# TensorE's order written by hand from the trunk to the first up tiles of an encoder layer

## The chip, the cores and the metric

The kernel runs on one core of one Trainium2 chip. The metric is the device time of one execution in microseconds (us); the time of a version is the median of its runs. An engine executes its own queue in order; queues wait for each other through semaphores.

## What is computed

One layer of a hybrid streaming encoder for 1024 prompt frames and 32 sample frames, model width 1024, all in float32:

```python
def trunk_layer(x, ...):                       # x: frames x 1024
    z = rms_norm(x, g_mix) @ w_in              # q, k, v, conv_h, conv_B, conv_C, gate_a, gate_b
    a = window_attention(q, k, v) @ w_attn_out
    bo = (cb * causal_conv3(cc * ch)) @ w_conv_out
    x = x + (sigmoid(ga) * a + sigmoid(gb) * bo) @ w_mix_out
    cq = rms_norm(x, g_cross) @ w_cq           # 4 heads x 64, 256 memory tokens
    x = x + softmax_attention(cq, mem_k, mem_v) @ w_co
    x = x + square(relu(rms_norm(x, g_mlp) @ w_up)) @ w_down
    return x                                   # then a final rms_norm
```

`rms_norm(x, g)` is `x * rsqrt(mean(x*x) + 1e-6) * g`.

## The kernel before

**Layout and precision.** Activations lie transposed: 128 features on the partitions, frames along the free axis. The 1056 frames are cut into three chunks `CH` of 384, 384 and 288 frames, called c = 0, 1, 2 here. Every float32 operand is split in two float32r parts, hi and lo; a product is then three matmuls (hi·hi, hi·lo, lo·hi) for each of 8 feature blocks, 24 matmuls in `gemm`. A weight tile (128 x 1024) is loaded raw into `wr`, its hi part `wh` is copied by ScalarE (ACT), its lo part `wl` is subtracted by VectorE (DVE). Outputs go to PSUM: three `acc` tiles, two `pt` tiles, one `s` and one `o`.

**Weights.** `plan` is a list of items; `worder` is the order of their weights. `next_w` keeps up to three split weights ahead. `fetch_w` lets SyncE (SP) load the raw tile; there are two `wr` tiles, so a load waits until the tile two before it has been split. From the trunk on each weight is used once per chunk, so three times. For every second tile of `w_conv_out`, `w_mix`, `w_cq`, `w_co` and `w_up` (the dictionary `kept`, 14 tiles) the lo part is written to DRAM (`wl_d`) by a DMA from ACT's queue when it is first made, and loaded back the two later times instead of being subtracted anew.

**Order of the work around the change.** For chunk c the trunk is 16 products: `do_conv_out(c, f)` for f = 0..7, whose results are split into `mg` (tiles M), and `do_mix(c, f)` for f = 0..7, which adds to the residual `x1`, makes the operands of the cross attention (`gain_split`), and adds the squares up in `accs[c]` (`square_acc`, on GpSimd, POOL). Beside the trunk of chunk c+1 runs the cross attention of chunk c, in small steps: statistics (`chunk_stats`), two products `do_cq`, for each head `scores`, `turn` (transposes of the probabilities) and `values`, then `do_co` in two halves, and statistics again. The statistics are two parts: `stats_col` sums the squares with TensorE (into `pq`) and takes the inverse root on DVE and ACT; `stats_row` builds diagonal matrices on ACT (L207) and DVE (L208) and spreads the result over the partitions with TensorE (`pr`, L209 and L210); ACT copies it to `R[c]`. The cross attention of chunk 2 runs beside the up products of chunks 0 and 1 (`up0(0) + up0(1)`); then come the up products of chunk 2 for the first 8 of 32 hidden blocks. Chunks 0 and 1 are normalised ahead of the up products (`normed_split`); chunk 2's up products take the raw rows, and `R[2]` is multiplied in when the product leaves PSUM. The other 24 hidden blocks are done in 12 pairs (`up_pair`), which multiply two chunks and two blocks with seven half products on sums of operands (`combine_n`, `combine`); the raw weights of a pair are `r1` (in `wr`) and `r2` (in `wr2`, two tiles). At last comes the down product.

`beside(steps, fillers, late)` interleaves: after each filler product one step of the cross attention is put. It sets the order in the program's text. The order in each engine's queue is then set by a scheduler at build time, which goes through the program with estimated durations and gives an engine the first instruction, by place in the text, whose inputs are there by then: a matmul of a later product may come ahead of a statistic that is not ready by the estimate. Only the loads at the start are exempt (`manual_schedule` for SP).

Of the kernel before, what the change touches and what calls it, by code (L numbers as in the profile page):

```python
# [10 lines left out]
F32 = mybir.dt.float32  # L11
F32R = mybir.dt.float32r
AF = mybir.ActivationFunctionType
ALU = mybir.AluOpType
# [4 lines left out]
P = 128  # L19
# [4 lines left out]
NF = 8  # L24
KV = 4
EPS = 1e-6
NCT = 6


G_MIX, G_CROSS, G_MEM, G_MLP, G_FIN = 0, 8, 16, 24, 32  # L30
# [8 lines left out]
def hybrid_step(ctx: ExitStack, tc: tile.TileContext, io):  # L39
# [5 lines left out]
    def nm(s):  # L45
        uid[0] += 1
        return f"{s}_{uid[0]}"
# [12 lines left out]
    wp = ctx.enter_context(tc.tile_pool(name="wp", bufs=3))  # L60
# [29 lines left out]
    def tmp(n, dt=F32):  # L90
        return tp.tile([P, n], dt, tag="ct", bufs=NCT, name=nm("ct"))

# [10 lines left out]
    def item(fn, *keys):  # L103
        plan.append((fn, keys))
        worder.extend(keys)
# [18 lines left out]
    fetched = []  # L124

    def fetch_w():
        raw = wp.tile([P, 1024], F32, tag="wr", bufs=2, name=nm("wr"))
        sp.dma_start(raw, weight(worder[wpos[0] + len(fetched)]))
        fetched.append(raw)

    def issue_w():
        if not fetched:
            fetch_w()
        raw = fetched.pop(0)
        key = worder[wpos[0]]
        hi = wp.tile([P, 1024], F32R, tag="wh", name=nm("wh"))
        lo = wp.tile([P, 1024], F32R, tag="wl", name=nm("wl"))
        if kept.get(key) is not None:
            sp.dma_start(lo.bitcast(F32), kept[key])
            act.copy(hi, raw)  # L140
# [81 lines left out]
    def chunk_stats(c):  # L222
        chunk_col(c)
        chunk_row(c)
# [711 lines left out]
    def hidden(c, j, h):  # L936
        sp.dma_start(hid_d[c][:, j], h)

    def up_part(w, c, j):
        n = CH[c][1]  # L940
        a = ps.tile([P, n], F32, tag="pt", bufs=2, name=nm("pa")) if w[0] == "late" else acc_tile([P, n])
        gemm(a, w[-2:], xm[c])
        t = tmp(n)
        if c == 2:
            dve.scalar_tensor_tensor(t, a, 0.0, R[c], op0=ALU.max, op1=ALU.mult)  # L945
        else:
            dve.tensor_scalar_max(t, a, 0.0)
        h = tmp(n)
        pool_e.tensor_tensor(h, t, t, op=ALU.mult)
        hidden(c, j, h)  # L950

    def do_up(j, c):
        return (lambda w: up_part(w, c, j)), ("w_up", j)


    comb = {}
# [34 lines left out]
    raws, wset = {}, {}  # L991

    def pair_fetch(key, src1, src2):
        r1 = wp.tile([P, 1024], F32, tag="wr", bufs=2, name=nm("wr"))
        r2 = L["pool"].tile([P, 1024], F32, tag="wr2", bufs=2, name=nm("wr2"))
        sp.dma_start(r1, src1)
        sp.dma_start(r2, src2)
        raws[key] = [r1, r2]

    def pair_issue(key, which):  # L1000
        r1, r2 = raws[key][:2]
# [28 lines left out]
    def up_fetch(i):  # L1030
        if i < len(UP):
            pair_fetch(("u", i), io["w_up"][UP[i][0]], io["w_up"][UP[i][1]])

    def up_issue(i, which):
        if i < len(UP):
# [100 lines left out]
        return x  # L1136


    def cross_steps(c):
        units = [Cross(c, h) for h in ([0, 1, 2, 3] if c < 2 else [4, 0, 1, 2, 3])]  # L1140
        nu = len(units)
        steps = [("call", [mem_load] if c == 0 else [mem_load_s] if c == 1 else [])]
        steps.append(("call", [lambda: chunk_stats(c)]))
        steps.append(("items", [(do_cq(c, j), ("w_cq", j)) for j in range(2)]))
        for i in range(nu + 2):
            calls = []
            if i < nu:
                calls.append(units[i].scores)
            if 0 <= i - 2 < nu:
                calls.append(units[i - 2].values)  # L1150
            if 0 <= i - 1 < nu:
                calls.append(units[i - 1].turn)
            steps.append(("call", calls))
            if c < 2 and i < nu:
                steps.append(("call", []))
        if c == 2:
            steps.append(("call", [open_late]))
            steps.append(("call", []))
            steps.append(("call", []))
        steps.append(("items", [(do_co(c, 0), ("w_co", 0))]))  # L1160
        steps.append(("items", [(do_co(c, 1), ("w_co", 1))]))
        steps.append(("call", [lambda: chunk_stats(c)]))
        return steps

    def beside(steps, fillers, late=()):
        for i, filler in enumerate(fillers):
            item(*filler)
            for x in [x for at, x in late if at == i]:
                item(lambda x=x: x())
            if steps:  # L1170
                kind, what = steps.pop(0)
                for x in what:
                    if kind == "items":
                        item(*x)
                    else:
                        item(lambda x=x: x())
        return steps

    def trunk(c):
        return [(do_conv_out(c, f), ("w_conv_out", f)) for f in range(NF)] + [  # L1180
# [6 lines left out]
    left = beside([], trunk(0))  # L1187
    left = beside(cross_steps(0), trunk(1))

    normed = lambda c, at: [(at + i, lambda f=f: normed_split(c, f)) for i, f in enumerate((0, 4, 1, 5, 2, 6, 3, 7))]  # L1190
    left = beside(left + cross_steps(1), trunk(2), normed(0, 6))
    left = beside(left + cross_steps(2), up0(0) + up0(1), normed(1, 0) + [(4, lambda: combine_n(0)), (6, lambda: combine_n(1)), (8, lambda: combine_n(2)), (9, lambda: combine_n(3))])
    assert not left
    for j in range(NF):
        item(*do_up(j, 2))
        if j < 4:
            item(lambda j=j: combine(j))
        if j == 5:
            item(lambda: [up_fetch(0), up_fetch(1), up_issue(0, 1)])
        if j == 6:  # L1200
            item(lambda: [up_issue(0, 2), up_issue(1, 1)])


    worder.append(STOP)
# [67 lines left out]
    def final_last(c):  # L1272

        n = CH[c][1]
        for f in range(NF):
            act.mul(x1[c][f], x1[c][f], col(G_FIN + f))
        chunk_col(c)
        row = stats_row(BLOCKS[c], n, RC[c])
        r = misc.tile([P, n], F32, tag=f"R{c}", name=nm("R"))
        act.copy(r, row)  # L1280
        at = 0
        for k, tag in ((1, "wr"), (2, "wh"), (2, "wl"), (3, "wr")):
            y = wp.tile([P, k, n], F32, tag=tag, bufs=2 if tag == "wr" else 3, name=nm("y"))
# [135 lines left out]
```

## Time and profile before

| | before |
|---|---|
| median of 3 runs | 1846.12 us (1845.42 to 1847.79) |
| profiled execution, time | 1845.38 us |
| profiled execution, span from first to last instruction | 1843.6 us |
| TensorE busy, matmuls | 1802.2 us, 11364 |
| VectorE, ScalarE, GpSimd busy | 1048.8, 720.6, 363.1 us |
| mean granted TensorE clock | 0.993 |

Engines in the profile: PE is TensorE, PEld its weight loads, DVE is VectorE, ACT ScalarE, POOL GpSimd, SP SyncE; a trailing q is the engine's sequencer. L166 is line 166 of the kernel. In the view by stages a row is a stretch of time in us from the span's start; its columns are the length, the busy time of PE, PEld, DVE, ACT and POOL with the number of instructions, the mean granted clock of TensorE as a share of full speed, the busy share of the DMA engines and GB/s. In the timeline a row is start, duration, engine, line, operation, written tile <- read tiles, count, and in brackets the idle time of the engine before it and who ended it.

In the trace the trunk of chunk 0 runs from about 816 to 884 us, that of chunk 1 to about 972, that of chunk 2 to about 1066, the up products of chunks 0 and 1 to about 1169, those of chunk 2 to about 1202; the pairs follow.

### The profile page before, as it was taken

To read this page: it belongs to the slowest core of one execution; us is meant where nothing else is said; L and a number is where in the kernel's file an instruction comes from. 1 tells how busy PE (TensorE), PEld (TensorE's weight loads), DVE (VectorE), ACT (ScalarE), POOL (GpSimd) and SP (SyncE) were. 2 spreads that over 40 slices of the span, in tenths; PEclk is the share of its full clock that TensorE was granted. 3 is DMA by queue.
4 is the path that set the end of the run, shared out by engine and by line. 5 is a ranking of instruction groups with operands and counts; after the bars stand their busy time and mean duration, and the time that the engine had idled before them with its cause. 6 is when DMAs were issued, how large, how long until landed. Compare 5 with 4: busy or idle time off the path is not lost.

```text
span 1843.6 us, 29554 instructions
## 1 busy us (share of the span) xinstructions
PE 1802.2 (98%) x11364; PEld 1785.2 (97%) x11364; DVE 1048.8 (57%) x2011; ACT 720.6 (39%) x1414; POOL 363.1 (20%) x381
## 2 busy tenths in 40 slices
PE   7999999999999999999999999899999999999997
PEld 7999999999999999999999999799999999999997
DVE  7766767757664223336675967646555664242255
ACT  7643435435344102323555746522222443030134
POOL 3211010201100000004333333463443000000023
PEclk9999999999999999999999999899999999999999
DMA  4411111212123124236755767733232674131244
GB/s 176 140 64 59 62 55 59 70 56 70 56 94 106 58 94 149 73 121 226 248 186 202 244 213 236 265 124 105 100 108 86 205 234 142 45 116 46 70 142 147
DMA packets 113933, 232.76 MB, mean 126 GB/s; under 512 B 13536, under 2 KB 76672, under 8 KB 113664
## 3 DMA queue, kind: packets, MB, share of 16 engines
q1 hardware_dynamic: 109472, 220.38, 36.0%
q10 hardware_dynamic: 4320, 10.49, 1.5%
q8 instruction: 90, 1.47, 0.3%
q14 instruction: 51, 0.42, 0.1%
HBM read 184.34 MB, written 46.48 MB: 125 GB/s over the span
## 4 chain that ended last, share of the span: by engine, by line
PE 89%; DVE 4%; DMA 3%; ACT 2%; issue 2%; SPq 0%; POOL 0%; POOLq 0%; DVEq 0%; ACTq 0%
PE acc L166 22%; PE acc L167 22%; PE acc L168 22%; PE acc L1024 3%; PE acc L1025 3%; PE acc L1026 3%; PE pt L535 1%; PE pa L168 1%; PE pa L167 1%; PE pa L166 1%; DVE wl L115 1%; PE sc L510 1%; PE sc L509 1%; PE o L548 1%; PE o L547 1%
## 5 line engine op out<-in xcount | busy, mean ns | idle before, releaser
L114 ACT CAST wh<-wr 128x1024 fp32r<-128x1024 f32 x200 | 210.6, 1053 | 485.6 <-PE acc L167 381.8
L166 PE MATMUL acc<-X,wh 128*128 128x384 f32 (+1 forms) x1200 | 391.0, 326 | 8.5 <-ACT wh L114 8.0
L167 PE MATMUL acc<-X,wh 128*128 128x384 f32 (+1 forms) x1200 | 388.1, 323 | 0.9 <-DVE X L241 0.9
L168 PE MATMUL acc<-X,wl 128*128 128x384 f32 (+1 forms) x1200 | 387.0, 323 | 0.3 <-DVE wl L115 0.3
L166 PE MATMUL acc<-Y,wh 128*128 128x384 f32 (+1 forms) x1008 | 330.2, 328 | 7.6 <-DVE ct L945 4.1
L167 PE MATMUL acc<-Y,wh 128*128 128x384 f32 (+1 forms) x1008 | 329.2, 327 | 0.0
L168 PE MATMUL acc<-Y,wl 128*128 128x384 f32 (+1 forms) x1008 | 328.8, 327 | 0.0
L115 DVE TENSOR_TENSOR wl<-wr,wh 128x1024 fp32r<-128x1024 f32 x200 | 268.4, 1342 | 78.7 <-ACT wh L114 77.8
L166 PEld LDWEIGHTS acc<-X,wh 128*128 128x128 f32 x1200 | 226.5, 189 | 9.2 <-ACT wh L114 8.0
L167 PEld LDWEIGHTS acc<-X,wh 128*128 128x128 f32 x1200 | 226.6, 189 | 2.7 <-DVE X L241 2.1
L168 PEld LDWEIGHTS acc<-X,wl 128*128 128x128 f32 x1200 | 226.4, 189 | 0.8 <-DVE wl L115 0.8
L166 PEld LDWEIGHTS acc<-Y,wh 128*128 128x128 f32 x1008 | 192.6, 191 | 9.0 <-DVE ct L945 4.3
L167 PEld LDWEIGHTS acc<-Y,wh 128*128 128x128 f32 x1008 | 192.4, 191 | 0.0
L168 PEld LDWEIGHTS acc<-Y,wl 128*128 128x128 f32 x1008 | 192.2, 191 | 0.0
L237 POOL TENSOR_TENSOR xacc<-xacc,ct 128x384 f32<-128x384 f32 (+1 forms) x62 | 82.2, 1329 | 358.0 <-ACT ct L235 355.5
L166 PE MATMUL acc<-M,wh 128*128 128x384 f32 (+1 forms) x320 | 104.8, 329 | 1.7 <-DVE Gb L761 1.7
L168 PE MATMUL acc<-M,wl 128*128 128x384 f32 (+1 forms) x320 | 104.5, 327 | 0.6 <-DVE wl L115 0.6
L167 PE MATMUL acc<-M,wh 128*128 128x384 f32 (+1 forms) x320 | 104.4, 327 | 0.2 <-DVE M L115 0.2
L747 POOL TENSOR_TENSOR ct<-ct,ld 128x384 f32<-128x384 f32 (+1 forms) x21 | 23.8, 1138 | 372.0 <-DVE ct L746 344.4
L1135 DVE TENSOR_TENSOR Gb<-acc,Gb 128x384 f32<-128x384 f32 (+1 forms) x60 | 31.4, 523 | 111.2 <-PE acc L168 111.2
L114 ACT CAST PTh<-pt 128x512 fp32r<-128x512 f32 (+3 forms) x94 | 45.9, 518 | 122.8 <-PE pt L535 122.0
L166 PE MATMUL acc<-H,wh 128*128 128x288 f32 (+1 forms) x256 | 80.7, 315 | 0.0
(292 smaller groups left out, 3482.6 us busy)
## 6 DMA issues: line engine op xcount, KB each, us to landing
wr<-in_w_down SPq DMA_DIRECT2D x56, 512.0 KB, 3.3
wr<-in_w_in SPq DMA_DIRECT2D x50, 512.0 KB, 3.2
wr<-in_w_up SPq DMA_DIRECT2D x48, 512.0 KB, 3.8
wl<-wl_d SPq DMA_DIRECT2D x28, 512.0 KB, 4.4
wr<-in_w_conv_out SPq DMA_DIRECT2D x24, 512.0 KB, 4.5
wr<-in_w_mix SPq DMA_DIRECT2D x24, 512.0 KB, 4.6
ct<-hid_d SPq DMA_DIRECT2D x64, 192.0 KB, 3.8
hid_d<-lt SPq DMA_DIRECT2D x48, 192.0 KB, 1.8
```

Of the source, the lines that this page charges most:

```text
L114: act.copy(hi, src)
L115: dve.tensor_sub(lo, src, hi.bitcast(F32))
L166: pe.matmul(out, wh[:, a], hi, start=(k == 0), stop=False)
L167: pe.matmul(out, wh[:, a], lo, start=False, stop=False)
L168: pe.matmul(out, wl[:, a], hi, start=False, stop=(k == len(acts) - 1))
L237: pool_e.tensor_tensor(acc, acc, sq, op=ALU.add)
L509: pe.matmul(sc[:, h, j * w : j * w + w], q[h], a, start=True, stop=False)
L747: (dve if f == NF - 1 else pool_e).tensor_tensor(t, t, t1, op=ALU.add)
L1024: pe.matmul(acc, wh[:, a], hi, start=(start and k == 0), stop=False, skip_group_check=True)
L1025: pe.matmul(acc, wh[:, a], lo, start=False, stop=False, skip_group_check=True)
L1026: pe.matmul(acc, wl[:, a], hi, start=False, stop=(k == 3), skip_group_check=True)
L1135: dve.tensor_add(x, a, x)
```

## The change

- TensorE's queue is taken out of the scheduler's hands from the first product of the trunk to the last of the first 24 up products (`manual_schedule` for PE): there it follows the text. The other engines are ordered by the scheduler as before.
- `beside` and the lists of steps are replaced by one list of 56 fillers (the trunks of chunks 1 and 2, and the up products of chunks 0, 1 and 2) and a table `after_filler`, which says by number what comes after which filler. Chunk c's cross attention starts at filler 0, 16, 32.
- The two parts of a statistic stand one filler apart (`chunk_col` after filler 0, 16, 32, 48; `chunk_row` after 1, 17, 33, 49), where `chunk_stats` had them together. After 16 and 32 two chunks have their parts together.
- `values` comes one filler after `turn` for every head; for chunks 0 and 1 it was two fillers for the first three heads. `turn` comes two fillers after `scores`; for chunk 2 it was one. Chunk 2's five heads start after fillers 35, 36, 38, 39 and 41 (they started after 35 to 39).
- `normed_split(0, f)` stands after fillers 18 to 25 (it was 22 to 29), `normed_split(1, f)` after 34 to 39 (32 to 39), `combine_n` after 40 to 43 (36 to 41), `combine` after 49 to 52 (48 to 51).
- The first two up products of chunk 2 leave their PSUM tiles only after `R[2]` is there (`all_waiting`); their matmuls don't wait for it.
- Raw weights have three tiles (`NWR`) in place of two, in the whole kernel. In the pairs `r1` and `r2` share those three; `wr2` keeps one tile for the first pair, loaded earlier (`up_first`).
- The 14 lo parts are written to DRAM from SP's queue in place of ACT's.

```diff
+NWR = 3
...
-        raw = wp.tile([P, 1024], F32, tag="wr", bufs=2, name=nm("wr"))
+        raw = wp.tile([P, 1024], F32, tag="wr", bufs=NWR, name=nm("wr"))
...
-                act.dma_start(kept[key], lo.bitcast(F32))
+                sp.dma_start(kept[key], lo.bitcast(F32))
...
-    def up_part(w, c, j):
+    def up_part(w, c, j, wait=False):
         n = CH[c][1]
         a = ps.tile([P, n], F32, tag="pt", bufs=2, name=nm("pa")) if w[0] == "late" else acc_tile([P, n])
         gemm(a, w[-2:], xm[c])
+        def rest():
+            t = tmp(n)
+            if c == 2:
+                dve.scalar_tensor_tensor(t, a, 0.0, R[c], op0=ALU.max, op1=ALU.mult)
...
+        if wait:
+            waiting.append(rest)
         else:
+            rest()
...
-        r1 = wp.tile([P, 1024], F32, tag="wr", bufs=2, name=nm("wr"))
-        r2 = L["pool"].tile([P, 1024], F32, tag="wr2", bufs=2, name=nm("wr2"))
+        r1, r2 = (wp.tile([P, 1024], F32, tag="wr", bufs=NWR, name=nm("wr")) for _ in range(2))
...
+    def up_first(step):
+        if step == 0:
+            L["rest"] = pair_fetch_first(("u", 0), io["w_up"][UP[0][0]], io["w_up"][UP[0][1]])
+        else:
+            L["rest"]()
...
+    def cross_steps(c, base, starts, co_at, stats_at):
         units = [Cross(c, h) for h in ([0, 1, 2, 3] if c < 2 else [4, 0, 1, 2, 3])]
+        at(base, lambda: chunk_col(c))
+        at(base + 1, lambda: chunk_row(c))
+        for j in range(2):
+            at(base + 2, (do_cq(c, j), ("w_cq", j)))
+        for i in range(base, base + 16):
+            for lag, step in ((3, "values"), (2, "turn"), (0, "scores")):
+                if i - base - lag in starts:
+                    at(i, getattr(units[starts.index(i - base - lag)], step))
+        for j in range(2):
+            at(base + co_at + j, (do_co(c, j), ("w_co", j)))
+        at(base + stats_at, lambda: chunk_col(c))
+        at(base + stats_at + 1, lambda: chunk_row(c))
...
+    in_order = tc.manual_schedule(engines={mybir.EngineType.PE})
+    item(lambda: in_order.__enter__())
+    for filler in trunk(0):
+        item(*filler)
+    at(0, mem_load)
+    cross_steps(0, 0, [3, 5, 7, 9], 13, 16)
+    at(16, mem_load_s)
+    cross_steps(1, 16, [3, 5, 7, 9], 13, 16)
+    cross_steps(2, 32, [3, 4, 6, 7, 9], 13, 16)
+    at(44, open_late)
+    at(49, all_waiting)
+    for i, f in enumerate((0, 4, 1, 5, 2, 6, 3, 7)):
+        at(18 + i, lambda f=f: normed_split(0, f))
+        at((34, 35, 35, 36, 37, 37, 38, 39)[i], lambda f=f: normed_split(1, f))
+    for k in range(4):
+        at(40 + k, lambda k=k: combine_n(k))
+        at(49 + k, lambda k=k: combine(k))
+    at(50, lambda: up_first(0))
+    at(53, lambda: [up_first(1), up_fetch(1), up_issue(0, 1)])
+    at(54, lambda: [up_issue(0, 2), up_issue(1, 1)])
+    run_fillers(trunk(1) + trunk(2) + up0(0) + up0(1) + up0(2))
+    item(lambda: in_order.__exit__(None, None, None))
```

More of the change, by code (lines that the diff above doesn't have):

```diff
@@ L998, in pair_fetch, with pair_fetch_first, rest @@
         raws[key] = [r1, r2]
+    def pair_fetch_first(key, src1, src2):
+        r2 = L["pool"].tile([P, 1024], F32, tag="wr2", name=nm("wr2"))
+        sp.dma_start(r2, src2)
+        def rest():
+            r1 = wp.tile([P, 1024], F32, tag="wr", bufs=NWR, name=nm("wr"))
+            sp.dma_start(r1, src1)
+            raws[key] = [r1, r2]
+        return rest
     def pair_issue(key, which):
@@ L1136, in down_part, with at @@
         return x
-    def cross_steps(c):
+    after_filler = {}
+    def at(i, *what):
+        after_filler.setdefault(i, []).extend(what)
+    def cross_steps(c, base, starts, co_at, stats_at):
         units = [Cross(c, h) for h in ([0, 1, 2, 3] if c < 2 else [4, 0, 1, 2, 3])]
[L1141 to L1163, printed above, removed]
@@ L1166, in beside, with run_fillers @@
+        at(base + stats_at, lambda: chunk_col(c))
+        at(base + stats_at + 1, lambda: chunk_row(c))
+    def run_fillers(fillers):
         for i, filler in enumerate(fillers):
             item(*filler)
[L1168 to L1176, printed above, removed]
@@ L1177, in beside @@
-        return steps
+            for x in after_filler.get(i, ()):
+                if isinstance(x, tuple):
+                    item(*x)
+                else:
+                    item(lambda x=x: x())
     def trunk(c):
@@ L1186, in hybrid_step @@
         kept.update(((name, j), None) for j in range(1, n, 2))
[L1187 to L1201, printed above, removed]
+    in_order = tc.manual_schedule(engines={mybir.EngineType.PE})
[20 more added lines that the diff above has]
+    item(lambda: in_order.__exit__(None, None, None))
     worder.append(STOP)
```

21 lines of the change are left out of this document (11 added, 10 removed).

## The prediction

> **What bounds the kernel now.** I read the page first, then the view by stages, then the waits of TensorE, then the timeline at its longest waits. From the page:
>
> ```profile
> span 1843.6 us, 29554 instructions
> PE 1802.2 (98%) x11364; PEld 1785.2 (97%) x11364; DVE 1048.8 (57%) x2011; ACT 720.6 (39%) x1414; POOL 363.1 (20%) x381
> ```
>
> TensorE works for all but 41.4 us of the span, and the change alters no matmul. So there is nothing to win but idle time and time at a lowered clock. The stages show where these lie (length, PE, PEld, DVE, ACT, POOL busy, granted clock, DMA share, GB/s):
>
> ```profile
> 0.00:816.00 816.00, 804.61 (x5179) 795.37 (x5180) 462.79 (x1081) 333.09 (x750) 85.49 (x154) 1.00 0.25 85
> 816.00:884.00 68.00, 67.24 (x381) 66.22 (x380) 43.54 (x55) 26.90 (x41) 26.77 (x19) 1.00 0.68 228
> 884.00:972.00 88.00, 88.00 (x525) 87.89 (x524) 60.46 (x102) 51.18 (x95) 25.83 (x23) 1.00 0.62 206
> 972.00:1066.00 94.00, 88.07 (x598) 86.80 (x597) 67.85 (x132) 58.65 (x115) 35.46 (x33) 0.96 0.65 218
> 1066.00:1169.00 103.00, 97.34 (x588) 94.00 (x587) 75.69 (x145) 56.95 (x124) 36.24 (x29) 0.98 0.74 250
> 1169.00:1202.00 33.00, 26.83 (x163) 25.96 (x164) 20.08 (x33) 14.47 (x24) 18.88 (x17) 0.84 0.74 238
> 1202.00:1240.00 38.00, 36.38 (x234) 35.82 (x233) 18.14 (x21) 9.42 (x12) 24.88 (x20) 1.00 0.30 99
> 1240.00:1843.60 603.60, 593.76 (x3708) 593.11 (x3706) 300.26 (x446) 169.91 (x258) 109.58 (x90) 0.99 0.36 119
> ```
>
> Length less PE is the idle time: 11.4 us before the trunk, 9.8 us in the last stage, and between them, where the order is now laid by hand, 0.8 + 0 + 5.9 + 5.7 + 6.2 + 1.6 = 20.1 us. The clock is below full only where idle time is. Narrower stretches price that, and give the length of a product:
>
> ```profile
> 990.30:997.10 6.80, 6.78 (x24) 6.79 (x25) 5.77 (x17) 2.39 (x7) 2.39 (x3) 0.51 0.60 230
> 1080.30:1086.50 6.20, 6.14 (x32) 5.83 (x32) 2.99 (x11) 0.43 (x2) 0.86 (x1) 0.72 0.60 203
> 1170.00:1175.00 5.00, 5.00 (x29) 5.00 (x28) 3.51 (x4) 2.55 (x4) 2.72 (x3) 0.66 0.47 164
> 1185.40:1192.00 6.60, 6.60 (x29) 6.60 (x30) 5.59 (x9) 2.19 (x4) 6.10 (x6) 0.54 0.86 269
> 1048.00:1056.00 8.00, 4.94 (x33) 4.34 (x32) 7.94 (x13) 4.57 (x9) 6.77 (x4) 1.00 0.82 283
> 1194.60:1201.00 6.40, 6.40 (x50) 6.40 (x50) 3.55 (x5) 2.94 (x4) 5.46 (x6) 1.00 0.93 293
> 819.60:836.50 16.90, 16.90 (x98) 16.90 (x97) 11.79 (x15) 7.29 (x11) 5.07 (x4) 1.00 0.66 214
> ```
>
> Each of the first four follows a wait. The clock cost them 6.8 x 0.49 + 6.2 x 0.28 + 5.0 x 0.34 + 6.6 x 0.46 = 3.3 + 1.7 + 1.7 + 3.0 = 9.7 us. The fifth is a wait with DVE busy for 7.94 of 8.00 us. The last two hold nothing but products (a count includes matmuls cut by the ends): two of 24 matmuls of 288 columns in 6.4 us and four of 384 columns in 16.9 us. So a product covers 3.2 or 4.2 us.
>
> All that can be won is 20.1 + 9.7 = 29.8 us. Who ends the waits:
>
> ```profile
> PE pr L209 <- ACT ct L207: 7.8, 4, 2.8
> PE acc L166 <- DVE ct L945: 4.1, 1, 4.1
> PE acc L166 <- ACT Y L240: 1.9, 1, 1.9
> PE acc L166 <- DVE Gb L761: 1.7, 1, 1.7
> ```
>
> The longest kind is the spreading half of the statistics (one of its four is at the kernel's end and stays).
>
> **The statistics, set a product apart.** The chain with a table load, then one without:
>
> ```profile
> 985.76 0.72 PE L191 MATMUL pq<-ones,xacc 128*128 128x1 f32 x6
> 986.67 1.28 ACT L194 ACT_TABLE_LOAD   x1
> 989.01 0.16 DVE L199 TENSOR_TENSOR rc<-st_y,st_t 128x3 f32<-128x3 f32 x1
> 990.32 0.69 PE L209 MATMUL pr<-ct,ones_r 128*128 128x384 f32 x1 [2.80 <-ACT ct L207]
> 990.78 1.54 DVE L208 SCALAR_TENSOR_TENSOR ct<-ident,rc,ct 128x128 fp32r<-128x128 f32 x2
> ...
> 1077.00 0.72 PE L191 MATMUL pq<-ones,xacc 128*128 128x1 f32 x6
> 1080.30 0.44 PE L209 MATMUL pr<-ct,ones_r 128*128 128x384 f32 x1 [1.94 <-ACT ct L207]
> ```
>
> From the end of `pq` to L209: 3.8 us (986.5 to 990.3), or 2.6 (1077.7 to 1080.3); L210 waits for the last L208, at 992.3, so up to 5.8 us. The scheduler had put 7 and 3 matmuls in between. Now a whole product lies there, 4.2 us after fillers 0 and 32, 3.2 after 16 and 48. I take half of what the longest chain exceeds the cover by, as half of the four places (rows 17 and 33) have two chunks' chains on the same DVE and ACT: (5.8 - 4.2) / 2 = 0.8 us at rows 1 and 33, (5.8 - 3.2) / 2 = 1.3 at rows 17 and 49, together 4.2, between 0 (the fast chain everywhere) and twice that, 8.4. Queued behind a waiting L209 or L210 on TensorE is the next product, and behind that everything that reads it.
>
> The column half now comes one product after the last `do_mix`, and needs its square on POOL:
>
> ```profile
> 884.14 0.33 PE L166 MATMUL acc<-Y,wh 128*128 128x384 f32 x1
> 887.59 1.01 POOL L237 TENSOR_TENSOR xacc<-xacc,ct 128x384 f32<-128x384 f32 x1 [2.10 <-ACT ct L235]
> ```
>
> The next product starts at 884.14, the sum is there at 888.60, 4.5 us later: 0.3 us over the cover at fillers 0 and 32, 1.3 at 16, together 1.9 us.
>
> **The last statistic, and a third raw tile.** The 4.1 us wait:
>
> ```profile
> 1177.99 0.33 SPq L128 DMA_DIRECT2D wr<-in_w_up  x1
> ...
> 1183.29 1.05 ACT L140 CAST wh<-wr 128x1024 fp32r<-128x1024 f32 x1 [3.57 <-DMA wr<-in_w_up]
> 1184.36 0.40 ACT L220 COPY R<-pr 128x288 f32<-128x288 f32 x1
> ```
>
> `pr` was done at about 1181.3, but ACT stood for 3.57 us at a weight whose load left only when a second raw tile came free; the copy of R[2] was queued behind it, three filled `acc` tiles behind that copy. With three raw tiles the load leaves a product (3.2 us) earlier, which takes away 3.2 of 3.57; and one more product runs between `pr` and the first need of a fourth `acc`. I count this wait, the 1.9 us for L240 (a product now lies between `do_co` and its reader) and their clock as gone, but for 0.5 us.
>
> Elsewhere a third tile finds TensorE filled. At the start one SP wait goes; I take 0, bounds 1 us each way of the 11.4 us idle there. In the pairs `r2` now uses a tile that the previous pair's `r1` frees a pair earlier; that stage's idle time is its tail alone (9.8 us), so cost 0; without this cover one landing in each of 12 pairs.
>
> **Spills by SP.**
>
> ```profile
> wr<-in_w_conv_out SPq DMA_DIRECT2D x24, 512.0 KB, 4.5
> ...
> wl_d<-wl ACTq DMA_DIRECT2D x14, 512.0 KB, 4.8
> ```
>
> ACT loses 14 issues that waited for DVE; SP, on which every raw load, `ld` and output waits its turn, gets them. The bytes are the same. If each spill held the next load for its 4.8 us, the third tile's lead (4.2) would leave 0.6 x 14 = 8.4 us; without the lead 14 x 4.8 = 67, which needs raw loads without any slack; the stage with most spills (816 to 884) idles for 0.8 us, so they have some. I take 0, and 8.4 as the far end.
>
> **Steps moved.** `normed_split(0)`, 16 DVE operations, leaves the time about 1048 where DVE was the wait, for the time behind R[0]. But `values` has come a product closer to `turn`, and in that stage:
>
> ```profile
> 1031.01 0.49 PE L853 MATMUL pt<-ident,S 128*128 128x128 f32 x3
> ...
> 1036.80 1.00 DVE L115 TENSOR_TENSOR PTl<-pt,PTh 128x384 fp32r<-128x384 f32 x2
> ```
>
> The transposes end at about 1031.8 (this row and three more), the operands of `values` at 1037.8: 6.0 us where the new order covers 3.2. DVE needs 67.85 us of a stage that would shrink from 94 to 94 - 5.9 - 3.3 = 85, 80%. So I leave the 3.1 us of DVE waits (8.00 - 4.94 in the fifth stretch) as they are: bounds 0 and 4 heads x 2.8 = 11.2.
>
> **The sum.** Left over: 0.8 (816 to 884) + 1.9 + 4.2 + 0.5 + 3.1 + 1.6 (1202 to 1240) = 12.1 us; and, since waits of 1.94 us lowered the clock for 1.7 us, two such windows, 3.4. That is 15.5 of 29.8, so 14.3 us are won: 1845.4 - 14.3 = 1831.1 for the profiled execution (its span and 1.8 us around it); the median stands 0.7 higher, so 1831.8 us.
>
> The Trainium skill ("TensorE: Matmul & The Clock Gate", "HAM oscillation") says that only idle gaps above about 3.4 us bring TensorE back to half its clock. The rows differ: 2.80 and 1.94 us were enough. By that rule the 3.4 us of clock would not be left.
>
> **The rivals.**
>
> *Covered throughout.* All chains are of the fast sort and DVE keeps up. Left are 0.8 + 1.6 us: 27.4 won, 1818.7. For it: the fast chain exists, and the stage from 884 to 972 has no idle time with the steps in much this order. Against: DVE at 80%.
>
> *Waits stay but the clock does not fall*, as after the wait at 1048: 1831.8 - 3.4 = 1828.4. Against: three of four windows came behind waits under 3 us. (This is the skill's rule above.)
>
> *The spills hold up the raw loads:* 1831.8 + 8.4 = 1840.2. For it: raw loads and spills would share one queue. The skill ("DMA: Bandwidth & Descriptors", "Queues, rings and completion order") says that a DMA engine takes turns between queue rows; a spill on ACT's own row shared with the loads, on SP's it stands ahead of them. No run here shows it yet.
>
> *Given back in place.* The order changes which wait is seen, not its sum: DVE's backlog, with 72 to 73% busy from 972 to 1169, takes back what the statistics release. Between +3 and -3 us: 1846.
>
> *Slower: a queue that can't step aside.* Before, a late `values` let matmuls of the next product pass. Now TensorE stands. With 13 heads, each late by 2.8 us, 36.4 us, and the clock behind every third, 4 x 1.7 = 6.8, together 43.2 against 29.8: 1846.1 + 13.4 = 1859.5. It decides from a mean lateness of (29.8 - 6.8) / 13 = 1.8 us on. For it: 6.0 us at 1031. Against: in the 384-column stages the cover is 4.2, and 884 to 972 has no wait.
>
> That the change does nothing can be left out: the scheduler had split the statistics by 3 and 7 matmuls, the new order cannot.
>
> **How the numbers follow.** Chances: forecast 0.45 (its own range 1823 to 1839), covered 0.12, no clock loss 0.07, spills 0.06, given back 0.08, slower 0.22. A difference of 0.2%, 3.7 us, is about what a measurement of this kernel can tell from none. Faster: the first four, 0.70. The same: given back, 0.08. Slower: 0.22. The range leaves out most of the slower case and the edge of the covered one: 1818 to 1850.
>
> **What would show it.** Right: no `pr` wait above 2.2 us between 816 and 1240, the 4.1 us wait gone, at most two stretches with a lowered clock, `R` copied within 1.5 us of the last `pr`. Wrong: waits of PE on PTl or on `S` (L844) in trunk 2 summing to over 11 us, waits for `wr` loads, or SP waiting on L115 with a weight behind it; PE idle from 816 to 1240 above 20 us.

## The result, and the profile after

| | before | changed | ratio, 95% interval |
|---|---|---|---|
| median of 4 runs each, us | 1846.43 (1845.42 to 1847.79) | 1869.70 (1866.00 to 1871.64) | 1.0123 (1.0106 to 1.0141) |
| profiled execution, time / span, us | 1845.38 / 1843.6 | 1866.00 / 1864.2 | |

The change makes the kernel slower by 1.2%; the forecast was 1831.8 us, the range ended at 1850. Line numbers after the change stand one higher in the first part of the kernel (L210 and L211 are the two `pr` matmuls, L208 and L209 the diagonals); the residual addition after `do_co` is L906.

The page of the changed kernel, busy times of the engines:

```profile
span 1864.2 us, 29594 instructions
PE 1808.6 (97%) x11364; PEld 1787.9 (96%) x11364; DVE 1054.8 (57%) x2011; ACT 718.9 (39%) x1414; POOL 351.6 (19%) x381
```

As many matmuls and nearly the same instructions elsewhere: the 20.6 us are waits and clock. The view by stages from the trunk on, cut at the same times as before:

```profile
816.00:884.00 68.00, 65.19 (x353) 63.89 (x352) 42.08 (x54) 26.68 (x40) 26.20 (x17) 0.95 0.64 218
884.00:972.00 88.00, 84.28 (x500) 83.25 (x499) 57.55 (x95) 46.44 (x87) 23.28 (x20) 1.00 0.59 194
972.00:1066.00 94.00, 84.63 (x560) 81.27 (x560) 65.87 (x129) 56.00 (x112) 28.68 (x29) 0.98 0.64 209
1066.00:1169.00 103.00, 93.62 (x545) 90.57 (x545) 66.70 (x131) 52.19 (x111) 26.31 (x27) 0.93 0.60 200
1169.00:1202.00 33.00, 28.27 (x163) 27.21 (x164) 20.85 (x33) 17.44 (x30) 16.72 (x14) 0.90 0.70 238
1202.00:1240.00 38.00, 35.65 (x252) 34.82 (x252) 25.83 (x36) 15.30 (x25) 24.61 (x22) 1.00 0.67 225
```

Length less PE from 816 to 1240: 2.8 + 3.7 + 9.4 + 9.4 + 4.7 + 2.4 = 32.4 us idle, where it was 20.1. The stage from 884 to 972, which had no idle time at all, now has 3.7. Who ends TensorE's waits:

```profile
PE pr L210 <- ACT ct L208: 9.6, 6, 2.5
PE sc L837 <- ACT mkh L115: 3.5, 1, 3.5
PE co L902 <- DVE Gb L906: 3.3, 3, 2.1
PE o L873 <- DVE PTl L116: 3.1, 3, 1.5
PE acc L167 <- ACT M L115: 2.8, 3, 1.3
PE co L902 <- DVE Ga L906: 2.8, 3, 1.6
PE pq L192 <- DVE sum L282: 2.3, 1, 2.3
PE co L902 <- ACT Y L882: 2.1, 1, 2.1
```

The 4.1 us wait of before is gone. The rows of the statistics still wait, and there are kinds that the list of before didn't hold: `co` for the residual additions, `sc` for the sample keys. The lowered clock, six stretches from 816 to 1240:

```profile
857.20:864.03 6.83, 6.35 (x19) 5.96 (x20) 3.52 (x6) 2.02 (x4) 1.50 (x1) 0.50 0.67 243
1003.98:1007.39 3.41, 3.41 (x16) 3.41 (x15) 0.00 (x0) 0.48 (x1) 0.00 (x0) 0.50 0.30 108
1068.83:1072.24 3.41, 3.41 (x13) 3.41 (x12) 1.12 (x2) 0.80 (x2) 1.01 (x1) 0.50 0.38 130
1096.14:1099.55 3.41, 3.41 (x11) 3.04 (x11) 0.89 (x4) 1.43 (x5) 0.00 (x0) 0.50 0.75 275
1116.62:1123.45 6.83, 4.10 (x13) 3.93 (x14) 1.65 (x2) 3.44 (x10) 0.00 (x0) 0.50 0.46 154
1178.06:1184.89 6.83, 6.01 (x23) 5.66 (x24) 3.77 (x9) 3.83 (x8) 2.00 (x3) 0.50 0.93 333
```

TensorE worked 26.7 us in them at half speed, so 13.3 us are lost (9.7 before). Idle time and clock together are 45.7 us against 29.8, and the trunk begins 1.3 us later; of the 20.6 us about 3 are left without a place.

To compare many kernels, I use a length that depends on no cut: from the first trunk product to the first product of a pair. Timeline, first and last row of it, before, changed, and changed with TensorE free (below):

```profile
815.28 0.34 PE L166 MATMUL acc<-Y,wh 128*128 128x384 f32 x1
1201.70 0.41 PE L1024 MATMUL acc<-Y,wh 128*128 128x384 f32 x1 [0.34 <-DVE ct L945]
```

```profile
816.58 0.34 PE L167 MATMUL acc<-Y,wh 128*128 128x384 f32 x1
1222.02 0.41 PE L1050 MATMUL acc<-Y,wh 128*128 128x384 f32 x1
```

```profile
819.46 0.34 PE L167 MATMUL acc<-Y,wh 128*128 128x384 f32 x1
1188.87 0.34 PE L1050 MATMUL acc<-Y,wh 128*128 128x384 f32 x1
```

That is 386.4, 405.4 and 369.4 us. From there to the last matmul it is 635.5, 635.4 and 635.4: in these three kernels the pairs and the down product take equally long.

### The profile page after: what moved, and what is told of

It reads as the page before. It is cut to its first block, busy times and chain, and to the rows that moved or that the text cites. A ratio compares the mean times of both kernels' runs of the same rounds, so it can differ in the third digit from the quotient of the medians.

```text
span 1864.2 us, 29594 instructions
## 1 busy us (share of the span) xinstructions
PE 1808.6 (97%) x11364; PEld 1787.9 (96%) x11364; DVE 1054.8 (57%) x2011; ACT 718.9 (39%) x1414; POOL 351.6 (19%) x381
## 3 DMA queue, kind: packets, MB, share of 16 engines
q10 hardware_dynamic: 2304, 3.15, 0.5%
## 5 line engine op out<-in xcount | busy, mean ns | idle before, releaser
L1167 DVE TENSOR_TENSOR Gb<-acc,Gb 128x384 f32<-128x384 f32 (+1 forms) x60 | 31.4, 523 | 112.5 <-PE acc L169 112.5
```

Source lines behind the costliest of these rows:

```text
L1167: dve.tensor_add(x, a, x)
```

## The experiments

The theory after the result: the statistics gained what they should, and more was lost because a TensorE with a fixed order stands at every result that is late, where the scheduler's order had let other matmuls pass. Rivals: the queues of the loads (raw tiles, spills); and that only this order is a bad one. All runs, "stretch" being the length just defined and "idle" the part of it in which TensorE did nothing, both of the profiled execution; the ratio is to the kernel before on the same chip, so that ratios compare better than medians do. The profiled execution can lie some us off the median: 1866.0 against 1869.7 us in the changed kernel, 1869.3 against 1867.0 in e2_order.

| run | what differs | median us | ratio (95%) | stretch | idle |
|---|---|---|---|---|---|
| before | | 1846.4 | 1 | 386.4 | 18.5 |
| changed | | 1869.7 | 1.0123 (1.0106 to 1.0141) | 405.4 | 31.0 |
| e1_free | changed, TensorE free | 1830.9 | 0.9904 (0.9888 to 0.9921) | 369.4 | 10.1 |
| e8_before_pin | before, TensorE pinned | 1886.5 | 1.0219 (1.0196 to 1.0241) | 429.6 | 51.8 |
| e2_order | changed, raw tiles and spills undone | 1867.0 | 1.0101 (1.0086 to 1.0117) | 414.4 | 35.7 |
| e3_spill_act | changed, spills undone | 1866.8 | 1.0101 (1.0086 to 1.0116) | 405.5 | 31.1 |
| e7_free_raw | e1_free, raw tiles and spills undone | 1835.1 | 0.9942 (0.9925 to 0.9959) | 377.4 | 13.3 |
| e5_co | changed, co products placed otherwise | 1855.0 | 1.0039 (1.0024 to 1.0054) | 395.2 | 23.4 |
| e9_rows | e5_co, rows one product later | 1861.4 | 1.0091 (1.0066 to 1.0117) | 398.7 | 26.1 |
| e10_diag | e5_co, diagonals at the column | 1851.6 | 1.0025 (1.0015 to 1.0034) | 387.5 | 18.5 |
| e11_keys | e5_co, sample scores in two steps | 1856.4 | 1.0048 (1.0033 to 1.0063) | 392.6 | 23.7 |
| e12_all | e10_diag and e11_keys together | 1850.0 | 1.0012 (1.0002 to 1.0021) | 384.0 | 17.2 |
| e13_free_joint | e1_free, statistics together again | 1852.6 | 1.0031 (1.0020 to 1.0043) | 393.6 | 20.8 |
| e14_two | before, statistics in two steps | 1843.2 | 0.9980 (0.9971 to 0.9990) | 385.5 | 21.1 |
| e15_two_raw | e14_two, raw tiles and spills by SP | 1850.9 | 1.0021 (1.0007 to 1.0034) | 388.8 | 21.5 |
| e6_free_co | e1_free, co products placed otherwise | 1840.4 | 0.9972 (0.9950 to 0.9994) | 375.6 | 14.6 |

**Pinned or free, in both texts.** e1_free takes the three lines out that pin TensorE, e8_before_pin puts them into the kernel before:

```diff
-    in_order = tc.manual_schedule(engines={mybir.EngineType.PE})
-    item(lambda: in_order.__enter__())
...
-    item(lambda: in_order.__exit__(None, None, None))
```

> The changed kernel with TensorE's queue given back to the scheduler; text order, three raw tiles and spills by SP stay. Theory (TensorE, held in the written order, stands at steps that other matmuls went past before): the idle time of PE between 816 and 1240 us, 32 us in the changed kernel, falls to 20 or less, and the time to 1848 us or less. Rival (the spills in SP's queue and the sharing of raw tiles hold up loads, and so everything): within 5 us of the changed kernel's 1869.7 us.

> The kernel before, its own text, with TensorE kept in that text's order over the same region, and nothing else of the change. Theory (pinning itself costs, because every wait for DVE or ACT is then TensorE's own): all waits that the scheduler had filled come back, and here the statistics' row stands right behind its column, 4 to 5 us each for five of them, so it is slower than the changed kernel or near it: 1865 to 1895 us. Rival (what costs is this hand-laid order, not pinning; the order before is one that the scheduler hardly altered): 1846 to 1853 us.

Both theories held. Pinning costs 39 us in the changed text (2.2% by the ratios, 36.0 us of stretch) and 40 us in the text before (2.2%, 43.2 us). So it is not this order alone that is a bad one: both texts, each held in its own order, pay about the same. How much another fixed order pays, the runs with single places cured show below. In e8 the rows alone wait for 26.8 us; in the changed kernel, which sets them a product apart, for 9.6 (both with 2.5 us at the kernel's end, outside the stretch):

```profile
PE pr L209 <- ACT ct L207: 26.8, 7, 5.0
```

**The queues of the loads.** e3_spill_act gives the 14 spills back to ACT; e2_order, and e7_free_raw without the pin, undo the raw tiles too:

```diff
-NWR = 3
+NWR = 2
...
-                sp.dma_start(kept[key], lo.bitcast(F32))
+                act.dma_start(kept[key], lo.bitcast(F32))
...
-        r1, r2 = (wp.tile([P, 1024], F32, tag="wr", bufs=NWR, name=nm("wr")) for _ in range(2))
+        r1 = wp.tile([P, 1024], F32, tag="wr", bufs=NWR, name=nm("wr"))
+        r2 = L["pool"].tile([P, 1024], F32, tag="wr2", bufs=2, name=nm("wr2"))
```

> The changed kernel with the 14 spills on ACT's queue again, all else as changed. Theory (order): within 4 us of 1869.7. Rival (queues): 8 to 23 us faster, and the PE waits for M at about 855 us, 2.7 us in the changed kernel, gone.

> The changed kernel with two raw tiles and two wr2 tiles and with the spills on ACT's queue, as before the change; the written order of TensorE stays. Theory (order): 1863 to 1876 us. Rival (queues): below 1853 us.

> The changed kernel with TensorE given back to the scheduler, and besides the third raw weight tile and the spills by SP undone (two wr and two wr2 tiles, spills on ACT): what is left of the change is the order of the text alone, with the statistics in two steps products apart. Theory (the 16 us that the free version gains over the kernel before come from the order of the text, in which work stands between a statistic's column and its row): 1828 to 1834 us, since the same undoing moved the changed kernel by only -2.7 us. Rival (the gain is the third tile and the spills, which a free TensorE can use and a pinned one cannot): 1840 to 1847 us.

Undone under the pin they give 2.9 and 2.7 us, against a loss of 23; undone without it they cost 4.2 (e7 ends 1 us above its theory's range). The rival falls. For the third tile this is the rest of a gain and a loss: by the stretch it is worth 8.9 us under the pin (414.4 in e2 against 405.5 in e3) and, with the spills, 8.0 us without (377.4 against 369.4), and ACT's waits for loads of raw weights fall from 37 us in the kernel before to 3.7 in the changed one. What it gives there it loses again before and behind the stretch: the trunk begins at 814.3 us in e2 and at 816.2 to 819.9 in the pinned runs that have three tiles and the same start, and from the pairs on e3 takes 2.8 us longer than e2. VectorE in e1_free, TensorE behind it, then VectorE in e7_free_raw:

```profile
54.20 1.75 DVE L116 TENSOR_TENSOR wl<-wr,wh 128x1024 fp32r<-128x1024 f32 x1
55.87 0.97 DVE L282 TENSOR_TENSOR sum<-sum,sum 128x288 f32<-128x288 f32 x1
...
56.90 0.49 PE L192 MATMUL pq<-ones,sum 128*128 128x1 f32 x3 [2.31 <-DVE sum L282]
```

```profile
49.03 0.45 DVE L282 TENSOR_TENSOR sum<-sum,sum 128x288 f32<-128x288 f32 x1
49.40 1.21 DVE L116 TENSOR_TENSOR wl<-wr,wh 128x1024 fp32r<-128x1024 f32 x1
```

With three tiles the weight split runs ahead of the sum that TensorE waits for; with two it comes behind it. The trunk begins at 819.5 us in the one, at 815.3 in the other. That wait of 2.3 us is in the changed kernel and in e3 too, which have three tiles, and not in e2, which has two.

**One place: co.** A half of `do_co` makes four products: two in one PSUM tile of two banks, two in `acc` tiles. TensorE's second product into that tile waits until the first has been added to the residual. The second half of chunk 0 in the changed kernel, VectorE's rows and then TensorE's:

```profile
982.65 1.59 DVE L116 TENSOR_TENSOR wl<-wr,wh 128x1024 fp32r<-128x1024 f32 x1 [0.40 <-ACT wh L115]
984.16 0.55 DVE L906 TENSOR_TENSOR Gb<-co,Gb 128x384 f32<-128x384 f32 x1
...
982.36 0.34 PE L904 MATMUL co<-Y,wl 128*128 128x384 f32 x1
984.76 0.44 PE L902 MATMUL co<-Y,wh 128*128 128x384 f32 x1 [2.06 <-DVE Gb L906]
```

The first product ends at 982.7, a weight split takes VectorE until 984.2, the addition until 984.7. The kernel before and e1_free, where TensorE is free, have matmuls of the trunk in between, 21 in the first half and 25 in the second, and no wait. The first half's second product into that tile, before and in e1_free, each with the trunk matmul ahead of it:

```profile
967.08 0.33 PE L168 MATMUL acc<-M,wl 128*128 128x384 f32 x1
967.26 0.33 PE L901 MATMUL co<-Y,wh 128*128 128x384 f32 x1
```

```profile
974.08 0.33 PE L169 MATMUL acc<-M,wl 128*128 128x384 f32 x1
974.25 0.33 PE L902 MATMUL co<-Y,wh 128*128 128x384 f32 x1
```

e5_co keeps the pin and puts the two `acc` products between:

```diff
-                a = two[:, f % 4, :n] if f % 4 < 2 else acc_tile([P, n])
+                a = two[:, (f % 4) // 3, :n] if f % 4 in (0, 3) else acc_tile([P, n])
```

> The changed kernel with the four products of each half of do_co in another order of PSUM tiles: s bank 0, acc, acc, s bank 1, in place of s bank 0, s bank 1, acc, acc. Theory (order): the waits of the second product for the residual add of the first (6.1 us in six places, with up to 3 us of lowered clock behind them) go: 6 to 9 us faster than 1869.7. Rival (queues): the waits move to the next reader, within 2 us.

The six waits for L906 are gone; of the other kinds in the stretch only the waits of `values` for VectorE moved by more than half a us (from 3.1 to 1.5). By the medians the kernel is 14.7 us faster, more than the theory had. The stretch is 10.2 us shorter; it shows less than the medians, as the profiled execution lies below the median in the changed kernel and above it in e5_co (1857.6 against 1855.0 us).

**A second place: the rows.** In the changed kernel the rows wait at four places: 1.89 us (and 1.26 for the second diagonals), 1.94 (and 0.38 for the second chunk's row), 1.89, and 0.97 at the last. e9_rows is e5_co with one product more of cover:

```diff
-        at(base + 1, lambda: chunk_row(c))
+        at(base + 2, lambda: chunk_row(c))
         for j in range(2):
-            at(base + 2, (do_cq(c, j), ("w_cq", j)))
+            at(base + 3, (do_cq(c, j), ("w_cq", j)))
...
-    cross_steps(0, 0, [3, 5, 7, 9], 13, 16)
+    cross_steps(0, 0, [4, 6, 8, 10], 14, 16)
...
```

> The changed kernel, TensorE pinned, co products placed as in the run at 1855.0 us, and each statistic's row, with cq, scores, values and co behind it, one trunk product later (the last statistic's row stays). Theory (TensorE waits at the rows because ACT's queue has a weight cast ahead of the diagonals that itself waits for TensorE; a product more lets both pass): the five waits at the rows, 9.2 us in that run, go, less 1 to 3 us that come back at the later steps: 1846 to 1849 us. Rival (the waits move with the row, since the cast of the next weight stands there in the same way): 1853 to 1857 us.

The rival was right in kind: the rows wait 1.90, 1.94 and 1.89 us again. (The 9.2 us of the theory held the 2.5 us at the kernel's end, which could not go.) The time lies above both ranges: 6.4 us more than e5_co, 3.5 in the stretch, with new waits at the steps that were moved. ACT and TensorE of e9_rows:

```profile
1000.79 1.04 ACT L141 CAST wh<-wr 128x1024 fp32r<-128x1024 f32 x1 [1.30 <-PE acc L168]
1001.74 1.57 ACT L208 ACTIVATE ct<-ident,rc 128x128 fp32r<-128x128 f32 x5
...
1002.77 0.44 PE L210 MATMUL pr<-ct,ones_r 128*128 128x384 f32 x1 [1.94 <-ACT ct L208]
```

ACT stands idle for 1.30 us at a weight cast that waits for TensorE to finish with an old weight; the diagonals stand behind the cast; TensorE stands behind the diagonals. At both places that were tried, the same product that should cover the row is the one that holds up its operands: cast 1.04 + diagonals 0.9 = 1.94. What a cover is worth depends on what stands ahead in the other queue. e10_diag makes the diagonals in the column's step, so that the text has them ahead of that cast:

```diff
     def chunk_col(c):
         RC[c] = misc.tile([P, 3], F32, tag=f"rc{c}", name=nm("rc"))
         stats_col(accs[c], BLOCKS[c], RC[c])
+        diags[c] = stats_diag(BLOCKS[c], CH[c][1], RC[c])
...
```

> The changed kernel, TensorE pinned, co products placed as in the run at 1855.0 us, and each statistic's diagonals (ACT's products and DVE's differences) made at the column instead of at the row; the row's two matmuls stay where they are. In that run, and in the one with rows a product later, TensorE waited 1.9 us at each row: 1.04 us of a weight cast on ACT that itself begins when TensorE lets go of a weight tile, and 0.9 us of diagonals behind it. Theory (two queues in a fixed order wait for each other; the diagonals ahead of the cast break it): the four waits of 1.9 us in the middle go, with the half clock after two of them: 1844 to 1849 us. Rival (ACT's queue is laid by the scheduler's own estimate of when things are ready, which puts the cast ahead wherever the diagonals stand in the text): 1853 to 1857 us, with waits of 1.9 us.

ACT and TensorE of e10_diag, the diagonals now ahead of the cast:

```profile
1000.68 1.86 ACT L206 ACTIVATE ct<-ident,rc 128x128 fp32r<-128x128 f32 x6 [1.08 <-DVE st_t L199]
1002.46 1.03 ACT L141 CAST wh<-wr 128x1024 fp32r<-128x1024 f32 x1
...
1003.85 0.44 PE L214 MATMUL pr<-ct,ones_r 128*128 128x384 f32 x1 [0.81 <-DVE ct L207]
```

All waits of 1.9 us at the rows are gone, and the stretch is 7.7 us shorter than in e5_co: the theory's mechanism. The median moved by 3.4 us only and lies between the two ranges. The edit also changed the statistics of the start, which now make their diagonals before they claim a tile for `pr`; there a wait of 4.6 us stands where e5_co has one of 2.3, and the trunk begins at 823.3 us instead of 818.7:

```profile
PE acc L167 <- ACT ct L431: 4.6, 1, 4.6
```

**A third place, and all together.** In the changed kernel a sample key is loaded into the one raw tile `mkr` only when the key before it has been split; the scores stand at that for 1.1 and 3.5 us. e11_keys loads two keys ahead and takes the other two a product later:

```diff
+        if c == 2:
+            at(base + 1, units[0].early)
+            at(base + 4, units[0].scores2)
...
-    cross_steps(2, 32, [3, 4, 6, 7, 9], 13, 16)
+    cross_steps(2, 32, [3, 5, 6, 8, 9], 13, 16)
```

> The changed kernel, TensorE pinned, co products placed as in the run at 1855.0 us, and the sample head's scores in two steps: the first two keys loaded two trunk products ahead of their scores, the other two keys' scores one product later, the heads behind it shifted by one product. Theory: the waits of 1.1 and 3.5 us for the sample keys go, and with them the half clock of 6.8 us behind them, which costs 3.4 us: 8 us in all at the most, 1847 to 1851 us. Rival (each key's load and split wait for the one before it through the single raw tile, so the wait comes back at the second step): 1852 to 1857 us.

> Both of the edits before (diagonals at the column, sample scores in two steps) together on the pinned kernel with the co products placed. Theory (the loss of 39 us is a sum of single places where the fixed order runs into another engine's queue, each with its own cure): the gains add up, 1836 to 1843 us, which is faster than the kernel before. Rival (cured waits come back at the next place in the fixed order, and only a TensorE that may step aside goes faster): 1848 to 1856 us.

In e11_keys the wait came back at the second step, as the rival said (waits of TensorE):

```profile
PE sc L851 <- ACT mkh L115: 4.5, 1, 4.5
```

By its median e12_all lies in the rival's range, 7 us above the theory's; it has the start's wait of 4.6 us in it. By the stretch the cures do add up: 10.2 for co, 7.7 for the rows and 2.6 for the keys, each alone, are 20.5 us, and together they took 405.4 to 384.0, 21.4 us. So 21.4 us, where the pin cost 36.0, were got back by hand at single places (by one profiled execution of each kernel, and the 2.6 of the keys without their wait gone). For the other 14.6 us I found no one place. The waits left are of 1 to 4 us, at the sample keys, `values`, `co` and the first `do_mix`; whether they too can be cured was not tried.

**What gains, once TensorE is free.** e13_free_joint is e1_free with each row right behind its column; e14_two is the kernel before with each row a product later; e15_two_raw adds the third tile and the spills by SP to that; e6_free_co is e1_free with e5_co's placing.

```diff
-        at(base + 1, lambda: chunk_row(c))
+        at(base, lambda: chunk_row(c))
...
-        at(base + stats_at + 1, lambda: chunk_row(c))
+        at(base + stats_at, lambda: chunk_row(c))
```

```diff
-        steps = [("call", [mem_load] if c == 0 else [mem_load_s] if c == 1 else [])]
-        steps.append(("call", [lambda: chunk_stats(c)]))
...
+        steps = [("call", first + [lambda: chunk_col(c)])]
+        steps.append(("call", [lambda: chunk_row(c)]))
...
```

> The changed kernel with TensorE given back to the scheduler, and each statistic's row put right behind its column in the text again; the rest of the changed text, the third raw tile and the spills by SP stay. Theory (in the free version the 11 us that the text's order gains come from the statistics in two steps: 7.8 us of waits at rows before, 2.5 us there): they go back, 1838 to 1844 us. Rival (a scheduler that may step aside moves the row behind other work itself, and the gain is the order of heads and fillers): 1829 to 1834 us.

> The kernel before, TensorE left to the scheduler, two raw tiles, spills on ACT, its own order of heads and fillers, and one thing of the change alone: each statistic's row stands one trunk or up product behind its column (the first normalised split of the second chunk moves by one product with it). Theory (the statistics in two steps carry all of the gain of the free version, 21.7 us by the run that put them together again): 1826 to 1836 us, faster than the kernel before. Rival (they only repay what the changed order of heads costs a free TensorE, and in the order before a row finds cover anyway): 1842 to 1848 us.

> The run before (statistics in two steps in the kernel before, TensorE free) with the third raw weight tile and the spills by SP besides. Theory (as in the changed text: about 4 us lost in the start, where a weight split goes ahead of the first statistic's sum on VectorE, and 7 us won behind it): 1 to 5 us faster than the run before it, 1823 to 1833 us. Rival (the start's loss stays and the gain behind it was one of that order): 2 to 5 us slower than the run before it.

> The changed kernel with TensorE given back to the scheduler, and besides the four co products of a half placed first bank, two other tiles, second bank (as in the run that took 14.7 us off the changed kernel). Theory (what costs is a program order that cannot step round a wait): a free TensorE already steps round the residual additions, so the new placing adds nothing: 1829 to 1833 us, within 2 us of 1830.9. Rival (the additions hold TensorE in any order, the scheduler hid only part): half of the 14.7 us comes off here too, 1822 to 1826 us.

Without the two steps the free version loses 21.7 us, more than its theory had, and its rows wait for 9.6 us in place of 2.5 (both with the 2.5 us at the kernel's end). Of the 24.2 us that its stretch is longer, 10.7 are idle time, 7.1 of these at rows, and 9.0 lowered clock:

```profile
PE pr L210 <- ACT ct L208: 9.6, 4, 3.2
```

So the scheduler does not find that cover by itself. But the two steps alone, in the order before, gain 0.2% only, as the rival of e14_two had it; there the rows still wait for 7.5 us where the kernel before has 7.8, and there are two long waits, of 3.6 us for an addition in `conv_out`'s results and of 3.5 us for a turn:

```profile
PE pr L209 <- ACT ct L207: 7.5, 4, 2.5
```

The gain of 1.0% came only with the two steps and the changed order of heads and normalised splits together: the two steps alone gave 0.2%, and the changed order without them, with the third tile and the spills by SP, is 0.3% slower than before. Why they need each other I cannot show. e15_two_raw went the other way than the theory had it (7.7 us slower, more than its rival said), and e6_free_co missed both of its expectations (9.5 us slower; its eight executions lie between 1834 and 1848 us, wider apart than those of any other run): edits that their theories took for harmless moved this scheduled kernel by 0.4 and 0.7%.

The version to keep is e1_free, the changed kernel without the pin: 1830.9 us, ratio 0.9904, faster than both. Its three neighbours, one edit away each, lie at 0.9942 (e7), 0.9972 (e6) and 1.0031 (e13): how much of its gain would outlast a small edit is open.

## Why the prediction was wrong

**The step that failed is the sum's "left over".** It took the waits that the profile of before shows (20.1 us, and 9.7 of clock) as the whole stock, and asked only which of them go. With the pin, waits that the scheduler had filled are back on the list, and a profile of before cannot show these as waits, since there they were filled. e8_before_pin shows how many there were: 33 us more idle time in the stretch (51.8 against 18.5) with no other edit. Term by term, from 816 to 1240 in the changed kernel:

- **Rows, 4.2 us forecast, 8.3 found** (1.89 + 1.26 + 1.94 + 0.38 + 1.89 + 0.97). The cover was reckoned as product against chain; that the cover holds up the chain through ACT's queue (e9, e10) was not seen. Its sign of being right, no such wait above 2.2 us, held, and yet the term was half the size.
- **Columns waiting for POOL's sum, 1.9 us:** no such wait of the changed kernel is in the list. Too much by 1.9.
- **The last statistic, 0.5:** right in size. The 4.1 us wait and the 1.9 us for L240 are gone, and R[2]'s copy starts 0.1 us after the last `pr` (at 1206.0 us). But the third raw tile, from which the prediction argued this, was not needed for it: in e2_order, with two, both waits are gone as well.
- **VectorE's waits, 3.1 us, reckoned for `values`:** right in size, 3.1 (0.19 + 1.54 + 1.34). The 3.1 us in the profile of before were not at `values`, but 1.74 us at an addition to `conv_out`'s results and 1.32 at `co`.
- **Not in the sum at all: co, 9.9 us** (6.0 for the residual additions, 2.1 and 1.8 for the last head's operands), **the sample keys, 4.6, and, but for 0.2 us, the operands M of the first `do_mix`, 4.1** (chunks 0 and 2). With the rows, `values` and 1.4 us at the first pair (1.6 forecast for the last stage) this makes 31.4 of the 32.4 us of idle time. In the timeline of before the second products of `co` for chunk 0 stand 21 and 25 matmuls of the trunk behind the rest of their halves; that order, read beforehand, would have shown what the pin takes away.
- **Clock, 3.4 forecast, 13.3 found**, since more waits are left. The rule of the Trainium skill, by which 3.4 us would have been saved ("TensorE: Matmul & The Clock Gate", "HAM oscillation": idle gaps above about 3.4 us), fared worse still: one of TensorE's waits between 816 and 1240 is longer than that, 3.50 us, and there are six stretches at half clock, where the prediction allowed two. The idle time, 32.4 us, is above the 20 us that it named as a sign of being wrong.
- **The start, 0 within 1 us:** the trunk begins 1.3 us later here, 4 us later in e1_free, where a stretch of 3.41 us at half clock (1.7 us) follows the 2.3 us wait. The third tile's idle cover was argued from loads; what it moved was a split on VectorE.
- **Spills, 0, far end 8.4:** the run without them is 2.9 us faster, the intervals overlap. The far end was not reached: TensorE waited for no `wr` load, ACT for three, 3.7 us in all. Whether the DMA engines take turns between queue rows (the Trainium skill, "DMA: Bandwidth & Descriptors", "Queues, rings and completion order") is not told by this, since hardly any raw load was late.

**Of the rivals** the one with a queue that can't step aside was right in kind and had 0.22. It was priced at one place, `values`, where 3.1 us were lost in place of 36; the loss came at rows, `co`, keys and `do_mix`, so its 1859.5 was too low and the range, cut below it, missed. That VectorE "takes back" the gain is not what happened: in the same times, 972 to 1169, it is less busy in the changed kernel than before, 65.87 + 66.70 against 67.85 + 75.69 us.

Setting the statistics apart did help: under a pin and with two raw tiles, it and the new order take the stretch from 429.6 (e8) to 414.4 us (e2). The forecast's size, 1831.8, is nearly that of e1_free; that is chance, since its terms are not those of that run: the forecast has neither the start's 4 us nor the waits for spilled parts (3.6 us in e1_free):

```profile
PE acc L169 <- DMA wl<-wl_d: 3.6, 3, 1.5
```

## What to carry to other kernels

Before an engine is taken out of a scheduler's hands, pin it in the old order as the first experiment: the profile of a scheduled kernel shows only the waits that the scheduler could not fill. A cover has to be reckoned through both queues: a step two products away still waits if its operands stand behind something that waits for the first of these products, and the cure is to put the operands ahead in the other queue, not the step further back. Where an order is to be changed, change the text and leave the scheduler its freedom, and take differences of half a per cent between such versions for the luck of the schedule until several neighbours agree.

## What was not expected of the hardware

From the trunk to the pairs the half clock comes in pieces of 3.41 and 6.83 us in the changed kernel, and the length of one wait does not settle whether it comes. Waits of 1.94 us (1000.05) and 1.89 us (1094.06) were each followed by a stretch at 0.50. Two waits of 1.89 and 1.26 us within 3.6 us, at 899.72, were not (the changed kernel, same columns as above):

```profile
899.70:907.00 7.30, 4.15 (x23) 3.88 (x23) 3.58 (x6) 2.73 (x6) 0.99 (x1) 1.00 0.61 209
```

TensorE is idle for 3.15 of these 7.30 us at full clock. In e5_co the same two waits, at 901.78 us, were followed by 3.41 us at 0.50. The 2.31 us wait of the start, too, was followed by no such stretch within 10 us in the changed kernel, by one of 3.41 us in e1_free (58.13) and by one of 6.83 us in e11_keys (55.85). What decides was not tried.
